# A two-layer hybrid encoder on one core: TensorE's instructions in the order they are emitted, mixer steps spaced by due times, a third PSUM bank for the dense products

## The chip, the cores and the metric

The kernel runs on one core of one Trainium2 chip. The metric is the device time of one execution in microseconds (us); lower is better. Before the change, three runs gave 3186.03, 3193.9 and 3196.83 us, median 3193.9 us. The engines are named as the profile names them: PE is TensorE's matmul, PEld its weight load, DVE VectorE, ACT ScalarE, POOL GpSimd, SP SyncE, which issues the DMAs.

## The reference

Two sequences (called b = 0 and 1 here) of 512 tokens with 1024 features go through two layers (l = 0 and 1) with shared weights. Cut to what matters:

```python
h = rms_norm(x, ln1_g[l])
z = h @ w_in[l]                                  # 1024 -> 2816, in four parts
y = s5(z_s5), hyena(z_hy), rwkv7(z_rw), na(z_na) # four mixers, 256 features each
x = x + concat(rms_norm(y_i, grp_g[l, i])) @ w_out[l]
h = rms_norm(x, ln2_g[l])
x = x + square(relu(h @ w_mlp1[l])) @ w_mlp2[l]  # 1024 -> 4096 -> 1024
```

S5 is a complex diagonal scan in both directions, Hyena two long convolutions done by DFT products, RWKV-7 a delta-rule scan in both directions, the fourth a softmax attention over a neighbourhood of a 8 x 64 grid. All is f32.

## The kernel before

**Dense products.** Features lie on the 128 partitions, the 512 tokens along the free axis. To keep f32 accuracy at the faster matmul type (fp32r), each operand is split into a rounded half `hi` and a rest `lo`, and each 128x128 weight block takes three matmuls of 512 columns (`mm3`, lines 1433 to 1435: hi times hi, hi times lo, lo times hi). A product of `w_in`, `w_out` or `w_mlp1` is 24 such matmuls into one PSUM tile, one of `w_mlp2` is 12. There are 9024 of them. Weights come in blocks of 256 KB through three `hi` buffers and four others (`load_w`): on the first use of a block (sequence 0) it is loaded, cast to `hi` on ACT (L300), the rest `lo` taken by a subtraction on DVE (L301) and written to DRAM; on the second use (sequence 1) block and rest are both loaded, and only the cast on ACT is left (L1417).

**Mixers.** The four mixers of each layer and sequence are many small f32 matmuls and transpositions on PE with chains of DVE, ACT, POOL and DMA work between them. In RWKV (`rw_step`) the longest such chain lies between the transpositions of line 506 and the 32x32 matmuls of line 564 (the inverse of a triangular matrix, lines 508 to 552, on DVE with DMAs in between); a shorter one between line 413 and the matmuls of line 470; then a loop of four serial steps (lines 636 to 687: pw, pu, pS, py). In Hyena (`hy_mixer`) the chain between the forward DFT (L1227) and the inverse (L1277) is the complex arithmetic of line 1196 on DVE and POOL.

**What sets the order.** The program is written as Python generators: one emits the dense stages in turn (w_in of both sequences, then for each layer and sequence w_out, the MLP, the next layer's w_in), two emit mixers. `together` steps them in turn: two steps of each mixer stream for each dense product. The emission order gives each instruction a priority; dense matmuls get a priority number worse by 2000 (`OFF_P`). A list scheduler, which has its own estimate of every instruction's duration, then fixes the order on each engine: it issues whatever it takes to be ready, best priority first. On the chip each engine runs its list strictly in that order.

**Dependences between stages.** w_out of (l, b) needs all four mixers of (l, b), normalised (`group_norm`), split into hi and lo (`take`). Mixers of (l, b) start when the RWKV part of its w_in is done; Hyena and the attention of (0,1), (1,0) and (1,1) start after RWKV and S5 of the same (l, b). After the last w_out only the MLP of (1,1) is left.

**PSUM.** Eight banks: two for dense products (`pd`), three for RWKV, later Hyena (`ra`), two for S5, attention and others (`ma`), one for the norms (`nm`).

## Time and profile before

| | |
|---|---|
| median of three runs | 3193.9 us (3186.03 to 3196.83) |
| profiled execution, its own time | 3182.62 us |
| its span, first to last instruction | 3180.8 us |
| PE busy | 2964.7 us, 93% |
| DVE, ACT, POOL busy | 1935.5, 1128.3, 453.6 us |
| mean granted clock of TensorE | 0.949 |

PE's busy time is the union of matmuls whose ends are modelled and overlap, so it is not PE at its peak. [...] The stages, by the first and last matmul of each: w_in of (0,0) and (0,1) to 469 us; no dense matmul from there to 550; w_out and MLP of (0,0) to 1166; w_in of (1,0) to 1334; w_out and MLP of (0,1), 1340 to 1949; w_in of (1,1) to 2118; w_out and MLP of (1,0), 2145 to 2749; w_out and MLP of (1,1), 2778 to 3176.

### The profile page before, as it was taken

The page shows a single profiled execution, that of the slowest core. Times are in us where ns is not written, and L with a number is a line of the kernel's source. Part 1 is how long each engine was busy: PE and PEld are TensorE (multiplying, and loading weights), DVE is VectorE, ACT ScalarE, POOL GpSimd, SP SyncE. Part 2 cuts the span into 40 slices and gives each one's busy share as a digit, 9 for nine tenths or more (in the row PEclk, how much of TensorE's full clock was granted, in tenths as well). Part 3 has the DMA queues.
Part 4 walks back from the last instruction along what each step waited for, and adds up shares of the span by engine and source line. Part 5 has one row for each costly group of instructions (what it writes and reads, how often), then busy time and mean ns, then how long its engine had stood idle before and what let it go on. Part 6 is the DMA issues. An engine that isn't in the chain of part 4 may idle for free. (4 is left out here: it accounts for less than half of the span.)

```text
span 3180.8 us, 48627 instructions
## 1 busy us (share of the span) xinstructions
PE 2964.7 (93%) x17328; PEld 2317.7 (73%) x17328; DVE 1935.5 (61%) x3909; ACT 1128.3 (35%) x2080; POOL 453.6 (14%) x411
## 2 busy tenths in 40 slices
PE   7978999899999999999999899988999999799999
PEld 5666776677777867777777677866777777588887
DVE  7987783874874697653844527668547467731223
ACT  4333233443332343244332324333433333343332
POOL 3422210200100022211101002213000001100000
PEclk9988997899999999999999999989999999899999
DMA  7577564464565566774764655666646555466666
GB/s 220 184 228 189 172 188 142 139 169 158 163 194 168 188 204 202 240 236 155 207 174 145 182 169 196 218 200 187 177 139 169 174 178 185 155 215 194 194 192 215
DMA packets 491801, 588.70 MB, mean 185 GB/s; under 512 B 188678, under 2 KB 239494, under 8 KB 490536
## 3 DMA queue, kind: packets, MB, share of 16 engines
q1 hardware_dynamic: 491560, 585.59, 60.1%
q8 instruction: 139, 2.28, 0.3%
q14 instruction: 102, 0.84, 0.1%
HBM read 418.34 MB, written 164.22 MB: 183 GB/s over the span
## 5 line engine op out<-in xcount | busy, mean ns | idle before, releaser
L1433 PE MATMUL pd<-m,m 128*128 128x512 f32 x2984 | 1222.0, 410 | 63.8 <-ACT m L300 23.4
L1435 PE MATMUL pd<-m,m 128*128 128x512 f32 x2984 | 1205.7, 405 | 22.5 <-DMA m<-lo 15.7
L1434 PE MATMUL pd<-m,m 128*128 128x512 f32 x2984 | 1205.8, 404 | 1.6 <-DVE m L301 1.4
L1433 PEld LDWEIGHTS pd<-m,m 128*128 128x128 f32 x2984 | 578.3, 194 | 214.2 <-ACT m L300 27.8
L1435 PEld LDWEIGHTS pd<-m,m 128*128 128x128 f32 x2984 | 577.9, 194 | 166.3 <-DMA m<-lo 19.5
L1434 PEld LDWEIGHTS pd<-m,m 128*128 128x128 f32 x2984 | 579.1, 194 | 131.2 <-issue 8.4
L300 ACT CAST m<-m 128x512 fp32r<-128x512 f32 (+1 forms) x400 | 256.4, 644 | 619.9 <-PE pd L1434 220.6
L1417 ACT CAST m<-m 128x512 fp32r<-128x512 f32 x376 | 232.2, 619 | 612.9 <-DMA m<-in_w_mlp 362.4
L301 DVE TENSOR_TENSOR m<-m,m 128x512 fp32r<-128x512 f32 (+1 forms) x400 | 303.1, 761 | 203.4 <-ACT m L300 198.1
L1596 DVE TENSOR_TENSOR m<-pd,m 128x512 f32<-128x512 f32 x224 | 153.9, 688 | 205.4 <-PE pd L1435 204.5
L1578 DVE SCALAR_TENSOR_TENSOR do<-pd,do 128x512 f32<-128x512 f32 x128 | 88.0, 687 | 202.4 <-ACT do L1577 201.9
L1196 DVE TENSOR_TENSOR m<-m,m 128x512 f32<-128x512 f32 (+1 forms) x224 | 125.6, 601 | 6.5 <-PE ma L1375 4.8
L301 DVE TENSOR_TENSOR m<-do,m 128x512 fp32r<-128x512 f32 x128 | 88.2, 689 | 50.0 <-ACT m L300 49.2
L300 ACT CAST m<-do 128x512 fp32r<-128x512 f32 x128 | 79.4, 621 | 98.7 <-DVE do L1578 98.5
L1577 ACT ACTIVATE do<-pd 128x512 f32<-128x512 f32 x128 | 75.9, 593 | 37.6 <-PE pd L1435 37.3
L668 POOL TENSOR_TENSOR rw_se<-rw_st,rw_ec 128x256 f32<-128x256 f32 x24 | 15.8, 659 | 484.1 <-DVE rw_st L669 361.9
L470 PE MATMUL ra<-m,m 64*128 64x128 f32 x512 | 63.1, 308 | 21.8 <-DVE m L454 10.3
L1196 POOL TENSOR_TENSOR m<-m,m 128x512 f32<-128x512 f32 x32 | 49.0, 1534 | 234.7 <-DVE m L1196 77.7
L1457 POOL TENSOR_TENSOR m<-m 128x512 f32<-128x512 f32 x40 | 59.8, 1494 | 152.9 <-ACT m L1456 150.9
L863 POOL TENSOR_TENSOR m<-m,s5p_i 128x256 f32<-128x256 f32 x64 | 61.7, 963 | 135.7 <-DVE m L865 71.4
L678 PE MATMUL ra<-m,m 128*64 128x64 f32 x512 | 78.8, 248 | 1.3 <-DVE m L653 0.9
L470 PEld LDWEIGHTS ra<-m,m 64*128 64x128 f32 x512 | 54.3, 206 | 34.9 <-issue 24.3
(363 smaller groups left out, 3505.6 us busy)
## 6 DMA issues: line engine op xcount, KB each, us to landing
m<-in_w_mlp SPq DMA_DIRECT2D x512, 256.0 KB, 2.9
lo<-m SPq DMA_DIRECT2D x376, 256.0 KB, 2.6
m<-lo SPq DMA_DIRECT2D x376, 256.0 KB, 2.7
m<-in_w_in SPq DMA_DIRECT2D x176, 256.0 KB, 3.2
m<-zr SPq DMA_DIRECT2D x36, 512.0 KB, 4.8
m<-in_w_out SPq DMA_DIRECT2D x64, 256.0 KB, 3.5
m<-in_xT SPq DMA_DIRECT2D x32, 256.0 KB, 4.3
zr<-do SPq DMA_DIRECT2D x32, 256.0 KB, 2.4
```

The costliest lines, as they stand in the source:

```text
L300: self.nc.scalar.copy(out=hi, in_=x)
L301: eng.tensor_tensor(out=lo, in0=x, in1=hi.bitcast(F32), op=SUB)
L470: nc.tensor.matmul(out=pm[q][:, ch - c2, c], lhsT=bk[c][h, ch].rearrange("p a b -> p (a b)"), rhs=ar[c][h, ch].rearrange("p a b -> p (a b) ...
L678: nc.tensor.matmul(out=py[b0:b0 + 64, d, c], lhsT=uv[:, ch, c, q], rhs=sr[:, ch, 2 * c + q], start=st is None, stop=True)
L1196: eng.tensor_tensor(out=o, in0=a, in1=b, op=op)
L1417: nc.scalar.copy(out=hi, in_=raw)
L1433: K.nc.tensor.matmul(out=ps, lhsT=wh, rhs=hh, start=(i == 0), stop=False)
L1434: K.nc.tensor.matmul(out=ps, lhsT=wh, rhs=hl, start=False, stop=False)
L1435: K.nc.tensor.matmul(out=ps, lhsT=wl, rhs=hh, start=False, stop=(i == n - 1))
L1577: nc.scalar.activation(out=r, in_=ps, func=AF.Relu)
L1578: nc.vector.scalar_tensor_tensor(out=r, in0=ps, scalar=0.0, in1=r, op0=MAX, op1=MUL)
L1596: nc.vector.tensor_tensor(out=a, in0=ps, in1=a, op=ADD)
```

## The change

From the first w_out on, the whole PE list is in the order in which the program emits it (`manual_schedule` for PE alone); the other engines are still ordered by the scheduler. What is emitted when is set by `pace`: a clock `K.pe.clock` adds 0.00044 us per column for a dense matmul, 0.00168 us per column for an f32 one and 0.11 us for a transposition. A mixer's `yield 6` now means that its next step is emitted no sooner than 6 us later on that clock. Between steps of mixers, one half of a dense product (12 matmuls, or a whole one of `w_mlp2`) is emitted. The numbers are written at every yield of the mixers, for instance 2 and 11 behind the two halves of RWKV's preparation, 6, 6, 6, 8, 8 and 14 in the long chain, 2, 2 and 2.5 in the serial loop, 6, 5, 5 and 9 in Hyena's arithmetic.

With that, S5, RWKV, Hyena and attention of one (l, b) are started as separate streams (attention after the last part of RWKV has begun, Hyena after RWKV), and steps are cut where one matmul group waits for another engine. Three of four weight subtractions go to POOL instead of DVE. PSUM: `pd` has three banks, `nm` is gone, and the norms of x use `pd`; they are now computed beside the first products of the stage that needs them, which wait for the scale.

```diff
+class PE:
+    def matmul(self, out, lhsT, rhs, **kw):
+        n = int(np.prod(rhs.shape[1:]))
+        self.clock += n * (0.00044 if rhs.dtype == F32R else 0.00168)
+        self.nc.tensor.matmul(out=out, lhsT=lhsT, rhs=rhs, **kw)
...
 def rw_step(K, l, par, g, zr, prep, y, st, M, beside):
...
-        yield
+        yield (2, 11)[c]
...
 def load_w(K, key):
...
-        K.split(hi, lo, raw, nc.vector)
+        K.split(hi, lo, raw, nc.vector if K.nw % LO_V == 0 else nc.gpsimd)
...
 def dense(K, key, h, tag="pd"):
-    w = [load_w(K, key + (kh,)) for kh in range(2)]
     ps = K.p([P, S], tag)
-    mm3(K, ps, [(w[k // 4][0][:, k % 4], w[k // 4][1][:, k % 4], h[k][0], h[k][1]) for k in range(8)])
+    for kh in range(2):
+        wh, wl = load_w(K, key + (kh,))
+        mm3(K, ps, [(wh[:, j], wl[:, j]) + h[4 * kh + j] for j in range(4)], kh == 0, kh == 1)
+        if kh == 0:
+            yield
     return ps
...
 class Stream:
     def step(self, K):
-        for _ in range(self.n):
-            if self.live:
-                K.tc.cur_priority += self.off
-                try:
-                    next(self.gen)
...
+        try:
+            self.ready = K.pe.clock + (next(self.gen) or 0.0)
+        except StopIteration:
+            self.live = False
...
+def pace(K, dense, ordered, *mixers):
+    region = None
+    while dense.live or any(s.live for s in mixers):
+        now = K.pe.clock
+        n = 0
+        for s in mixers:
+            if s.live and s.ready <= now:
+                s.step(K)
+                n += 1
+        if dense.live:
+            dense.step(K)
+        if K.pe.clock == now:
+            K.pe.clock += 0.5
+        if region is None and ordered():
+            region = K.tc.manual_schedule(engines={mybir.EngineType.PE})
+            region.__enter__()
...
-        together(K, Stream(first_stream(), FN, OFF_M), Stream(rwkv_stream(), MIX), Stream(ds, 1, OFF_D))
+        pace(K, Stream(ds), lambda: (0, 0, "out") in done, Stream(first_stream()), Stream(rwkv_stream()))
...
-TB = "nm"
+TB = "pd"
...
-BANKS = {"pd": 2, "ra": 3, "ma": 2, "nm": 1}
+BANKS = {"pd": 3, "ra": 3, "ma": 2}
```

Three places in the lists of the engines. In the changed kernel every matmul is issued from line 203 and every transposition from line 207; a row with 128x512 on a tile `pd` is dense.

**PE, the end of w_in of (1,1), before w_out of (1,0).** Before (the last row is the first matmul of w_out; `ra` with L1277 is Hyena's inverse DFT of (1,0), `ma` with L959 the start of S5 of (1,1)):

```order
L1435 MATMUL pd_20196<-m_18565,m_20191 128x512
L1277 MATMUL ra_16291<-m_15506,m_16238 128x128 x2
...
L296 MATMUL ma_16158<-c_eye_129,rsq_yma_16146 128x128 x4
...
L959 MATMUL ma_20413<-m_20386,m_20409 64x64 x8
L271 MATMUL ra_16361<-c_ones_131,m_16356 128x1 x4
L959 MATMUL ma_20517<-m_20386,m_20513 64x64 x8
L959 MATMUL ma_20634<-m_20386,m_20630 64x64 x8
L296 MATMUL ra_16380<-c_eye_129,rsq_yra_16368 128x128 x4
...
L959 MATMUL ma_20740<-m_20386,m_20736 64x64 x8
L1433 MATMUL pd_20336<-m_18953,m_20320 128x512
```

Now (the fourth row is the first matmul of w_out):

```order
L203 MATMUL pd_19729<-m_18474,m_19759 128x512
L203 MATMUL pd_19779<-m_18188,m_19780 128x512 x2
...
L203 MATMUL pd_19779<-m_18474,m_19799 128x512
L203 MATMUL pd_19832<-m_18995,m_19833 128x512 x2
L203 MATMUL pd_19832<-m_18995,m_19834 128x512
```

The mixer work that stood between the two dense stages has gone to earlier places among the dense matmuls; the stages now follow each other directly.

**PE, the end of the MLP of (1,0), before w_out of (1,1).** Before (L271 and L296 are the norm of a mixer's output):

```order
L1435 MATMUL pd_25333<-m_25136,m_25326 128x512
L271 MATMUL ma_22745<-c_ones_131,m_22740 128x1 x4
L1277 MATMUL ra_22905<-m_22100,m_22848 128x128 x2
...
L296 MATMUL ma_22764<-c_eye_129,rsq_yma_22752 128x128 x4
L271 MATMUL ra_22979<-c_ones_131,m_22974 128x1 x4
L296 MATMUL ra_22998<-c_eye_129,rsq_yra_22986 128x128 x4
L1433 MATMUL pd_25377<-m_25351,m_25365 128x512
```

Now (`ra_25143` and `ra_25181` are Hyena's inverse DFT):

```order
L203 MATMUL pd_25124<-m_25083,m_25117 128x512
L203 MATMUL ra_25143<-m_24008,m_25034 128x128 x2
...
L203 MATMUL pd_25164<-m_24644,m_25156 128x512 x2
...
L203 MATMUL ra_25181<-m_24008,m_25034 128x128 x2
...
L203 MATMUL pd_25309<-m_25083,m_25302 128x512
L203 MATMUL ra_25326<-c_ones_131,m_25244 128x1 x4
L207 MATMUL ra_25346<-c_eye_129,rsq_yra_25333 128x128 x4
L203 MATMUL pd_25367<-m_25353,m_25368 128x512 x2
```

The inverse DFT has moved ahead of five dense products; the two matmul groups of the last norm still stand together, with nothing dense between them or behind them before w_out.

**POOL, the MLP of (0,0), beside the serial loop of RWKV of (0,1).** Before (L668 waits for RWKV's state, L1038 and L1041 are S5's, L1317 the attention's):

```order
L668 TENSOR_TENSOR rw_se_7131<-rw_st_6990,rw_ec_6056 128x256
L668 TENSOR_TENSOR rw_se_7224<-rw_st_7129,rw_ec_6056 128x256
L1038 TENSOR_TENSOR m_7155<-m_7155,m_7154 128x1024
L1041 TENSOR_TENSOR m_7154<-m_7155,m_7154 128x1024
L1317 COPY m_7628<-m_7584 128x256 x4
```

Now (L326 is the subtraction that makes `lo` of a weight block, L699 the line that was L668, L1362 that was L1317):

```order
L326 TENSOR_TENSOR m_9794<-m_9795,m_9793 128x512
L699 TENSOR_TENSOR rw_se_9878<-rw_st_9710,rw_ec_7876 128x256
L326 TENSOR_TENSOR m_9846<-m_9847,m_9845 128x512
L326 TENSOR_TENSOR m_9908<-m_9909,m_9907 128x512
L1362 COPY m_9899<-m_9640 128x256 x4
L326 TENSOR_TENSOR m_9999<-m_10000,m_9998 128x512
L699 TENSOR_TENSOR rw_se_10029<-rw_st_9876,rw_ec_7876 128x256
```

282 of the 376 weight subtractions now stand in POOL's list, between instructions of the mixers.

## Rows read from the trace of the kernel before

**Rows 1.** Page, busy time of each engine.

```profile
PE 2964.7 (93%) x17328; PEld 2317.7 (73%) x17328; DVE 1935.5 (61%) x3909; ACT 1128.3 (35%) x2080; POOL 453.6 (14%) x411
```

**Rows 2.** Windows, two stretches: window, length, busy by engine, PEclk, DMA.

```profile
0.00:550.00 550.00, 486.14 (x3131) 367.14 (x3132) 416.02 (x938) 200.13 (x377) 143.49 (x139) 0.89 0.65 190
550.00:3181.00 2631.00, 2478.59 (x14198) 1950.56 (x14198) 1519.45 (x2971) 928.12 (x1703) 310.10 (x272) 0.96 0.60 184
```

**Rows 3.** Windows by stage, columns PE, PEld, DVE, ACT, POOL, PEclk, DMA, GB/s.

```profile
469.00:550.00 81.00, 72.35 (x715) 52.77 (x716) 34.54 (x87) 27.46 (x71) 4.65 (x7) 0.73 0.54 147
...
642.00:1166.00 524.00, 500.15 (x3215) 391.58 (x3214) 342.98 (x686) 182.95 (x346) 48.21 (x42) 0.98 0.59 177
1166.00:1340.00 174.00, 158.49 (x834) 125.57 (x832) 134.64 (x271) 64.00 (x118) 42.86 (x38) 0.99 0.67 214
...
2118.00:2145.00 27.00, 15.43 (x131) 14.20 (x129) 22.24 (x58) 6.71 (x9) 3.63 (x3) 0.67 0.58 180
...
2749.00:2778.00 29.00, 10.04 (x58) 9.26 (x56) 21.69 (x50) 5.53 (x7) 3.83 (x4) 0.67 0.33 115
...
2824.00:3181.00 357.00, 350.69 (x1549) 289.14 (x1547) 95.50 (x141) 119.12 (x201) 0.00 (x0) 1.00 0.62 198
```

**Rows 4.** Waits of PE from 550 to 3181: total us, times, longest.

```profile
PE ra L564 <- DVE m L551: 18.1, 6, 4.4
PE pd L1433 <- DVE do L1578: 14.3, 9, 2.8
...
PE ra L1277 <- DVE m L1196: 10.5, 3, 8.3
PE ra L470 <- DVE m L454: 10.3, 5, 6.3
...
PE ra L470 <- DVE m L453: 5.8, 3, 4.0
...
PE pd L1433 <- DVE m L1596: 4.8, 4, 3.0
PE pd L1435 <- DVE m L301: 3.0, 3, 1.2
...
PE ra L678 <- DVE m L653: 0.9, 1, 0.9
```

**Rows 5.** Windows, instructions on tiles pd alone: PE, PEld, DVE, ACT, PEclk.

```profile
550.00:3181.00 2631.00, 1971.38 (x7968) 1508.46 (x7968) 300.91 (x436) 94.50 (x160) 0.96 0.60 184
2824.00:3181.00 357.00, 349.85 (x1537) 287.72 (x1535) 61.42 (x89) 23.57 (x40) 1.00 0.62 198
```

**Rows 6.** Timeline before w_out of (1,1).

```profile
2770.18 1.86 PE L271 MATMUL ra<-c_ones,m 128*128 128x1 f32 x8 [5.86 <-DVE m L1534]
...
2777.92 1.22 PE L1433 MATMUL pd<-m,m 128*128 128x512 f32 x2 [2.65 <-ACT m L300]
```

**Rows 7.** Timeline, RWKV's long chain of (1,1), from L506 to L564.

```profile
2418.79 0.90 PE L506 MATMUL ra<-c_eye,m 64*128 64x64 f32 x15
2473.11 1.11 PE L564 MATMUL ra<-m,m 32*32 32x32 f32 x64 [2.14 <-DVE m L551]
```

**Rows 8.** Timeline, Hyena's arithmetic, from L1227 to L1277, twice.

```profile
1991.77 1.02 PE L1227 MATMUL ra<-m,m 128*128 128x256 f32 x4
2022.85 1.39 PE L1277 MATMUL ra<-m,m 128*128 128x128 f32 x11
2716.07 1.13 PE L1227 MATMUL ra<-m,m 128*128 128x256 f32 x4
2758.25 5.63 PE L1277 MATMUL ra<-m,m 128*128 128x128 f32 x32 [8.31 <-DVE m L1196]
```

**Rows 9.** Lines, weight subtraction on DVE; subtractions and sums of that size on POOL.

```profile
L301 DVE TENSOR_TENSOR m<-m,m 128x512 fp32r<-128x512 f32 (+1 forms) x400 | 303.1, 761 | 203.4 <-ACT m L300 198.1 <-DMA zn<-do 2.1 <-DMA lo<-m 1.7
L1457 POOL TENSOR_TENSOR m<-m 128x512 f32<-128x512 f32 x40 | 59.8, 1494 | 152.9 <-ACT m L1456 150.9 <-issue 2.0
L447 POOL TENSOR_TENSOR m<-m,m 128x512 f32<-128x512 f32 x16 | 29.9, 1871 | 14.4 <-DVE m L445 11.5 <-ACT m L431 2.9
```

More of the change, by code (lines that the diff above doesn't have):

```diff
@@ L708, in rw_bonus @@
     yield
+    for c in range(2):
+        p2 = K.p([P, S], "ra")
+        K.pe.matmul(out=p2, lhsT=K.bd, rhs=r[:, c], start=True, stop=True)
+        nc.vector.tensor_tensor(out=r[:, c], in0=p2, in1=v[:, c], op=MUL)
+    M.free(v)
+    yield
     gate = M([P, 2, S])
@@ L740, in rw_out @@
         nc.vector.tensor_tensor(out=y[:, c], in0=gate[:, c], in1=y[:, c], op=MUL)
-        yield
+    rv = rn.rearrange("p (a b c) -> p a b c", a=4, b=2)
+    yield from K.head_bcast([rv[:, :, c] for c in range(2)], M, "ra", finish)
     M.free(bonus, gate)
+    yield 4
 def s5_ops(K, l, M, tag):
@@ L979, in s5_front @@
         M.free(tb, *t)
-        for _ in range(2):
-            yield
+        yield 4
     t = M([P, 8, 128])
@@ L1122, in hy_spectra @@
             M.free(dec)
-        yield
+        yield 4
     M.free(h, lr, w3, ws)
+    yield 2
     pn = K.p([P, S], tag)
     for hf in range(2):
-        nc.tensor.matmul(out=pn, lhsT=K.ones, rhs=tot[:, hf * S:hf * S + S], start=hf == 0, stop=hf == 1)
+        K.pe.matmul(out=pn, lhsT=K.ones, rhs=tot[:, hf * S:hf * S + S], start=hf == 0, stop=hf == 1)
     M.free(tot)
@@ L1344, in weights @@
                 hs = slice(64 * h, 64 * h + 64)
-                nc.tensor.matmul(out=ps[h][:, i], lhsT=q[hs, n * P:n * P + P], rhs=k3[hs, :, span[n]:span[n] + 32],
+                K.pe.matmul(out=ps[h][:, i], lhsT=q[hs, n * P:n * P + P], rhs=k3[hs, :, span[n]:span[n] + 32],
                                  start=True, stop=True)
@@ L1476, in norm_rstd, with w_in @@
     K.nc.scalar.copy(out=r, in_=pb)
-    K.tc.cur_priority += OFF_R
-    return r
-def w_in(K, l, par, h, R, dst, tags):
+    out.append(r)
+def w_in(K, l, par, h, st, M, dst, tags):
     nc = K.nc
     zr, zd, zh, zn = dst
+    Rs = []
+    rs = norm_rstd(K, st, M, Rs)
+    next(rs)
     hp = [(t[:, 0], t[:, 1]) for t in h]
@@ L1519, in s5 @@
         nc.sync.dma_start(out=zd.rearrange("g c t n -> (g c) t n")[i * P:i * P + P], in_=o)
+    R, early = None, []
     for off, n, fn in ((8, 8, rw), (0, 2, s5), (2, 6, hy), (16, 6, na)):
         for i in range(n):
-            fn(i, dense(K, ('w_in', l, off + i), hp, tags.pop() if tags else "pd"))
+            ps = yield from dense(K, ('w_in', l, off + i), hp, tags.pop() if tags else "pd")
+            if R is None:
+                next(rs, None)
+                early.append((fn, i, ps))
+                if Rs:
+                    R = Rs[0]
+                    for f, j, p in early:
+                        f(j, p)
+            else:
+                fn(i, ps)
             yield
@@ L1534, in group_norm @@
     nc.vector.tensor_tensor(out=sq[0], in0=sq[0], in1=sq[1], op=ADD)
-    rn = K.token_rstd(sq[:1], S, K.ones[:, 0:1], 1e-6, tag, sc=1.0 / 256)
+    yield 6
+    rn = yield from K.token_rstd(sq[:1], S, K.ones[:, 0:1], 1e-6, tag, tag, sc=1.0 / 256)
     M.free(*sq)
@@ L1563, in w_out, with mlp @@
     M.free(*(ys.pop(g) for kh in khs for g in HALVES[kh]))
-def mlp(K, l, h, R2, xd, done, M):
+def mlp(K, l, h, st, xd, done, M):
     nc = K.nc
     hp = [(t[:, 0], t[:, 1]) for t in h]
-    hid, acc, xp = {}, [], []
+    hid, acc, xp, R2 = {}, [], [], []
+    rs = norm_rstd(K, st, M, R2, True)
+    next(rs)
     def first(f):
-        ps = dense(K, ('w_mlp1', l, f), hp)
+        ps = yield from dense(K, ('w_mlp1', l, f), hp)
         t = M([P, 2, S], F32R)
@@ L1607, in mlp @@
     for f in range(32):
-        first(f)
+        yield from first(f)
+        next(rs, None)
         yield
@@ L1643, in both @@
         for s in streams:
-            s.step(K)
-        yield
+            if s.live and s.ready <= K.pe.clock:
+                s.step(K)
+        yield max(0.0, min([s.ready for s in streams if s.live], default=0.0) - K.pe.clock)
+def pace(K, dense, ordered, *mixers):
[5 more added lines that the diff above has]
+            if s.live and s.ready <= now:
+                s.step(K)
+                n += 1
[6 more added lines that the diff above has]
+            region.__enter__()
+    if region is not None:
+        region.__exit__(None, None, None)
 def chain(*gens):
@@ L1695, in into @@
             ys[l, b] = {}
-            for i, _ in enumerate(w_in(K, l, pars[l], h, R, zs[l, b], FIRST[:] if l + b == 0 else None)):
-                if i == 7:
+            for i, _ in enumerate(w_in(K, l, pars[l], h, st, DM, zs[l, b], FIRST[:] if l + b == 0 else None)):
+                if i >= 15:
                     done.add(("zr", l, b))
-                    if b == 0 and l and len(ys[l - 1, 1]) == 4:
-                        take(l - 1, 1)
-                    if b == 1 and l and len(ys[l, 0]) == 4:
-                        take(l, 0)
+                    other = (l, 0) if b else (l - 1, 1)
+                    if l and len(ys[other]) == 4 and other not in taken:
+                        take(*other)
                 yield
@@ L1760, in na @@
             yield from na_mixer(K, l, pars[l], zs[l, b][3], y, M, tag)
[L1761 removed]
+            yield from group_norm(K, pars[l], 3, y, tag, M)
             ys[l, b][3] = y, M
```

318 lines of the change are left out of this document (170 added, 148 removed).

## The prediction

> **What bounds the kernel now.** I read the page's busy times first [rows 1]: PE is busy in 93% of the span, every other engine in 61% or less, so the order on PE decides. Then the windows. The change orders PE by hand only from the first w_out on, at 550 us, so I split the span there [rows 2]. Behind 550 lie 2631 us with PE busy for 2478.6: 152 us idle, and a granted clock of 0.96, which is 0.04 x 2631 = 105 us of clock withheld. These 257 us are what a better order can win; before 550 the scheduler still orders PE. The windows by stage show where it lies [rows 3]: the last stage, dense work alone, has no idle time beyond its tail and a clock of 1.00, the long MLP stages with mixers have 0.98, and two short stretches in front of a w_out have 0.67 with PE busy 15.4 of 27 and 10.0 of 29 us. The waits of PE name what ends the idle time [rows 4]: chains of DVE work inside the mixers (L564, L470, L1277) and dense matmuls that wait for a PSUM bank to be read (L1578, L1596).
>
> How long a dense matmul needs: 1537 in 349.85 us, 0.228 us each [rows 5]. All 7968 behind 550 would need 1814 us; they were busy for 1971 [rows 5]. The 157 us between are clock, changes between mixer and dense work, and waits too short to show as idle.
>
> **The change part by part.** The number of matmuls is the same in both lists, so only idle time, clock and placement count. Each term is for the time behind 550.
>
> *Stage ends, -29.* Before w_out of (1,0) mixers are left over; now nothing stands there. The stretch is 27 us, its PE work at full clock is 15.4 x 0.67 = 10 us and is paid elsewhere: -17. Before w_out of (1,1) the inverse DFT moves ahead of five dense products, but the last norm still stands alone: from its first matmul to w_out it took 7.7 us [rows 6], and I keep 10 of the 29; with 10.0 x 0.67 = 7 us of PE work that is -12. Bounds: -39 (nothing is left) and 0 (other work is late there).
>
> *Third bank, -16.* The dense matmuls waited 14.3 us for L1578 and 4.8 for L1596 [rows 4], 19 in all; a third tile hides them. The norms now take banks of this tag too, so I leave 3. Bounds -19 and +10.
>
> *RWKV's long chain, -18.* From the last transposition (about 2419.7) to the first L564 the chip needed 53.4 us, 2.1 of them idle [rows 7]. Between the two, PE's list held 188, 223, 174, 164, 200 and 192 dense matmuls in the six instances, 37 to 51 us at 0.228: too few, hence 18.1 us of waits in all six [rows 4]. Now it holds 216, 252, 228, 264, 240 and 264, 49 to 60 us, and up to 14 us of mixer matmuls besides. What is late next is the chain's own end, which has room. Bounds -18 and +20 (if the chain lasts 57 us).
>
> *RWKV's preparation, -12.* L470 waited 10.3 and 5.8 us [rows 4], 2 us each time. The PE work in front of it was 5 to 10 us and is now 10 to 13. Bounds -16 and 0.
>
> *Hyena's arithmetic, +10.* Two instances took 30 and 41 us from L1227 to L1277, the second with an 8.3 us wait [rows 8]; now the list holds 33 to 34 us of PE work there, six times. I take two instances late by 5. Bounds 0 and 6 x 7 = +42.
>
> *Serial loop, +8.* Between its steps stood 21 dense matmuls on average and now mostly 12, 2.7 us. The trace shows 0.9 us of wait behind L653 with the longer distance [rows 4]. With some 60 steps, and the row's 0.9 for one in seven, +8; bounds 0 and 60 x 0.9 = +54.
>
> *Subtractions on POOL, +10.* 282 move. One takes 0.761 us on DVE and would take about 1.494 as the POOL group of that shape does [rows 9], 0.73 more. That is hidden where the rest is ready in time: of all these, PE waited only 3.0 us for L301 in three places [rows 4]. I charge 0.73 us to fourteen of them; if that cover were gone it would be 282 x 0.73 = +206. In exchange DVE sheds 282 x 0.761 = 215 of its 1935 us, so the other bound is -20.
>
> [...]
>
> *Short waits and mixing, -25.* Before, a mixer's matmul could break into a product after any dense matmul; now only between halves. Of the 157 us above, about 80 are clock (0.04 x 1971). I take a third of the other 77. Bounds -60 and 0.
>
> *Clock, -45.* The two short stretches account for 0.33 x 56 = 18 of the 105 us; 87 are left. The stages in which PE waits little run at 0.98 and 0.99, the last at 1.00 [rows 3]. If all mixer stages, some 2230 us, came to 0.985, 33 of the 87 would stay: -54; new waits take 9 back. Bounds -87 and 0.
>
> *Before 550, 0 +- 20.* The emission differs, the scheduler still orders. 33 of the 44 subtractions of the first w_in leave a busy DVE, 416 of 550 us [rows 2], but S5's preparation now shares the dense banks.
>
> Sum: -29 - 16 - 18 - 12 + 10 + 8 + 10 - 25 - 45 = -117 us. Against the profiled execution's 3182.6 that is 3066; it ran 11 us faster than the median of the runs, 3193.9, from which the forecast is 3077.
>
> **The rivals.** *All waits gone.* Every chain has room and the clock follows: 142 of the 152 us, the 87 of clock and 10 of mixing go: 3193.9 - 239 = 2955. For it: six of six L564 waits are covered. Against: Hyena's 33 us stands against 41 measured, and the stretch from 469 to 550 has PE busy 72 of 81 us at a clock of only 0.73 [rows 3], so mixers alone keep it low. [...]
>
> *Late rests from POOL (slower).* POOL runs its list in order, and the subtractions now stand behind instructions that wait for RWKV's state. If the rest of a block comes late by 0.73 us each time, the dense work of sequence 0 pays: 206 in place of 10, which is 3077 + 196 = 3273. It decides from 117 / 282 = 0.4 us a block. Against: one block feeds 12 matmuls, 2.7 us, and four buffers give three of these as slack; POOL is busy in 14% of the span [rows 1].
>
> *Chains longer than their due times (slower).* Hyena late by 7 us six times and the loop by 0.9 in every step, +96 in place of 18, and the clock stays at 0.96 since PE waits as often: 3077 + 78 + 45 = 3200.
>
> *Gain eaten up.* Half of that: the old waits go, new ones of the same size come with the shorter distances in the loop, and the clock stays: about 3165.
>
> **How the numbers follow.** The forecast's case, 3020 to 3140: 0.5. All or most waits gone, below 3020: 0.2. Gain eaten up, 3140 to 3184: 0.1; to within 0.3% of 3193.9, which is about what a measurement of this kernel can tell from no change, 0.06. Slower 0.14: POOL 0.05, chains 0.09. Faster is 0.5 + 0.2 + 0.1 = 0.8. The range 2955 to 3195 leaves out little below and the slower cases above; the likeliest case alone has 3020 to 3140.
>
> **What would show it.** Right: no stretch without dense matmuls before w_out of (1,0), a short one before w_out of (1,1); L564 and L470 out of the list of waits; no dense matmul waiting for L1578's successor; PEclk behind the first w_out near 0.98; DVE busy some 200 us less, POOL some 420 more. Wrong: L1277's successor with waits of several us in most instances; dense matmuls of sequence 0 waiting for POOL; idle time behind the first w_out above 100 us; or a first w_out much later or earlier than 550.

## The result, and the profile after

The changed kernel takes 3324.6 us (median of four runs) against 3190.0 us for the kernel before beside it: a ratio of 1.042, 95% interval 1.0387 to 1.0453. It is 135 us slower, where the prediction had 117 us faster. The profiled execution has a span of 3323.3 us.

The page's busy times of the changed kernel, as in [rows 1]:

```profile
PE 2993.9 (90%) x17328; PEld 2327.0 (70%) x17328; DVE 1878.6 (57%) x3627; ACT 1138.8 (34%) x2084; POOL 820.6 (25%) x693
```

The number of matmuls is the same and PE is busy only 29 us longer; 113 of the 142 us between the spans are idle time. POOL has 367 us more. By the prediction DVE sheds 215 us with the moved subtractions; it shed 57, since its other work became slower.

The windows of the changed kernel, cut at its first w_out, which now starts at 606 us; they answer to [rows 2], with the same columns:

```profile
0.00:606.00 606.00, 512.55 (x3253) 381.88 (x3253) 428.44 (x938) 209.33 (x388) 200.99 (x179) 0.86 0.60 175
606.00:3323.00 2717.00, 2481.34 (x14076) 1945.14 (x14076) 1450.16 (x2690) 929.44 (x1697) 619.62 (x514) 0.93 0.58 178
```

The first w_out is 56 us later. Behind it PE is busy as long as before, but idle for 236 us instead of 152, and the granted clock is 0.93 instead of 0.96. The stages, as in [rows 3] (from the end of w_in of sequence 1 to the first w_out; the first MLP; the next w_in; the stretches without dense matmuls before w_out of (1,0) and of (1,1); the last stage):

```profile
512.00:606.00 94.00, 82.41 (x746) 58.57 (x745) 49.47 (x137) 34.06 (x88) 7.50 (x11) 0.72 0.39 104
731.00:1317.00 586.00, 534.48 (x3324) 413.98 (x3323) 353.95 (x642) 199.51 (x394) 205.65 (x180) 0.93 0.55 166
1317.00:1508.00 191.00, 165.87 (x656) 122.66 (x654) 112.96 (x160) 68.31 (x96) 81.23 (x63) 0.90 0.60 195
2299.00:2306.00 7.00, 0.69 (x4) 0.23 (x2) 6.93 (x5) 0.62 (x2) 2.10 (x2) 0.88 0.90 213
2909.00:2920.00 11.00, 2.75 (x16) 2.14 (x15) 7.84 (x19) 4.46 (x6) 0.00 (x0) 0.63 0.64 215
2971.00:3323.00 352.00, 346.13 (x1531) 285.83 (x1529) 93.81 (x138) 117.08 (x198) 0.00 (x0) 1.00 0.62 199
```

The first MLP and the w_in behind it went from 0.98 and 0.99 to 0.93 and 0.90. The stretches before w_out of (1,0) and (1,1), 27 and 29 us before the change, are 7 and 11 us. The last stage, dense work alone, is what it was. What PE waits for behind the first w_out, as in [rows 4] (all matmuls now have line L203, all transpositions L207):

```profile
PE ma L203 <- DMA m<-s_sB: 37.4, 12, 13.1
PE ra L203 <- DVE m L482: 24.0, 4, 7.5
PE pd L203 <- ACT m L325: 23.5, 12, 6.5
PE pd L203 <- DVE m L1515: 18.2, 7, 6.3
PE pd L203 <- DVE m L1666: 11.8, 4, 6.4
PE ma L203 <- DVE m L1397: 11.4, 3, 5.8
PE ma L203 <- POOL m L1079: 8.4, 3, 5.1
...
PE pd L203 <- POOL m L326: 6.1, 8, 1.5
```

The old waits are nearly gone, as forecast: no line names the last step of RWKV's long chain or Hyena's arithmetic, and the MLP's squaring (L1648) has one wait of 0.9 us. Others have grown or are new: S5's operator blocks from DRAM (s_sB), RWKV's preparation (L482), weights and x on their way to the dense products (L325, L1515), the attention's scores (L1397), the last step of S5's activation function on POOL (L1079). The first of them stood in the list of the kernel before too, as its third longest line, which [rows 4] leaves out:

```profile
PE ma L959 <- DMA m<-s_sB: 11.7, 5, 4.9
```

A simple measure serves for what follows: the time at which the n-th dense product starts (us from the span's start; one product here is one 128x512 matmul on a tile `pd` or `ra`: the 9024 dense ones, 16 of RWKV's and, where the third bank is shared, 8 of S5's). I counted it in the traces of the runs told below. Number 1152 lies in the first w_out, 3456 in w_out of sequence 1, layer 0.

```
product   before  changed  a_dve  a_dve_noorder  spacing_only  unspaced0_hyena  best_with_order
  768       357     349     353       355            350            350             355
 1152       594     695     688       665            646            615             658
 3456      1378    1574    1555      1502           1507           1455            1485
 7680      2865    3006    2974      2863           2878           2835            2973
 span      3181    3323    3291      3180           3194           3152            3290
```

By product 3456 the changed kernel is 196 us late, at the end 142: the loss falls into the first half, and the second half is 54 us faster than before.

### The profile page after: what moved, and what is told of

Its sections match the earlier page's. It is cut to its first block, busy times and chain, and to the rows that moved or that the text cites. A ratio compares the mean times of both kernels' runs of the same rounds, so it can differ in the third digit from the quotient of the medians.

```text
span 3323.3 us, 48638 instructions
## 1 busy us (share of the span) xinstructions
PE 2993.9 (90%) x17328; PEld 2327.0 (70%) x17328; DVE 1878.6 (57%) x3627; ACT 1138.8 (34%) x2084; POOL 820.6 (25%) x693
## 5 line engine op out<-in xcount | busy, mean ns | idle before, releaser
L203 PE MATMUL pd<-m,m 128*128 128x512 f32 (+2 forms) x9248 | 2309.4, 407 | 136.1 <-ACT m L325 38.0
L203 PEld LDWEIGHTS pd<-m,m 128*128 128x128 f32 (+2 forms) x9248 | 1745.1, 194 | 580.8 <-issue 51.4
L326 POOL TENSOR_TENSOR m<-m,m 128x512 fp32r<-128x512 f32 x282 | 390.4, 1385 | 800.0 <-ACT m L325 768.9
L325 ACT CAST m<-m 128x512 fp32r<-128x512 f32 (+1 forms) x400 | 257.6, 645 | 728.5 <-PE pd L203 332.3
L203 PE MATMUL ra<-m,m 32*32 32x32 f32 (+5 forms) x3448 | 267.6, 251 | 42.8 <-DVE m L482 24.0
L1666 DVE TENSOR_TENSOR m<-pd,m 128x512 f32<-128x512 f32 x224 | 153.8, 688 | 248.1 <-PE pd L203 247.7
L203 PE MATMUL ma<-m,m 128*64 128x128 f32 (+10 forms) x1584 | 196.5, 322 | 94.0 <-DMA m<-s_sB 37.4
L1648 DVE SCALAR_TENSOR_TENSOR do<-pd,do 128x512 f32<-128x512 f32 x128 | 88.2, 689 | 338.7 <-ACT do L1647 338.4
L203 PEld LDWEIGHTS ra<-m,m 32*32 32x32 f32 (+4 forms) x3448 | 201.6, 151 | 106.7 <-issue 47.2
L203 PEld LDWEIGHTS ma<-m,m 128*64 128x64 f32 (+4 forms) x1584 | 117.8, 159 | 149.2 <-issue 55.7
L326 DVE TENSOR_TENSOR m<-m,m 128x512 fp32r<-128x512 f32 (+1 forms) x118 | 100.0, 848 | 117.0 <-ACT m L325 112.1
L1236 DVE TENSOR_TENSOR m<-m,m 128x512 f32<-128x512 f32 (+1 forms) x224 | 147.2, 707 | 0.0
L326 DVE TENSOR_TENSOR m<-do,m 128x512 fp32r<-128x512 f32 x128 | 92.4, 722 | 64.2 <-ACT m L325 63.0
L325 ACT CAST m<-do 128x512 fp32r<-128x512 f32 x128 | 79.6, 622 | 105.6 <-DVE do L1648 105.3
L1515 DVE SCALAR_TENSOR_TENSOR m<-m,par,m 128x512 fp32r<-128x512 f32 x64 | 64.3, 1014 | 31.3 <-ACT m L1514 31.2
L1236 POOL TENSOR_TENSOR m<-m,m 128x512 f32<-128x512 f32 x32 | 48.9, 1529 | 110.0 <-DVE m L1236 68.1
L203 PE MATMUL ra<-m,rw_st 64*64 64x64 f32 x448 | 75.7, 251 | 0.0
L560 DVE TENSOR_TENSOR m<-m 128x1024 f32<-128x1024 f32 x32 | 66.0, 2063 | 11.2 <-DMA m<-m 5.3
```

The costliest lines, as they stand in the source:

```text
L203: self.nc.tensor.matmul(out=out, lhsT=lhsT, rhs=rhs, **kw)
L325: self.nc.scalar.copy(out=hi, in_=x)
L326: eng.tensor_tensor(out=lo, in0=x, in1=hi.bitcast(F32), op=SUB)
L560: nc.vector.tensor_tensor(out=tm, in0=x[:, i:i + 4].unsqueeze(2).to_broadcast([P, 4, 16, 16]), in1=z.rearrange("p j k -> p k j").unsqueeze ...
L1236: eng.tensor_tensor(out=o, in0=a, in1=b, op=op)
L1515: nc.vector.scalar_tensor_tensor(out=h[:, 1], in0=x, scalar=g, in1=h[:, 0].bitcast(F32), op0=MUL, op1=SUB)
```

## Experiments

Ratios are to the kernel before on the same chip, with 95% intervals; "changed" is the changed kernel. Times in us are medians. The kernel before took 3183 to 3196 us on the chips used, so a difference between runs on two chips can be some us off; where that matters it is taken from the ratios.

### The parts, undone one by one

**a_dve**: the subtractions of the weights back on VectorE.

```
-LO_V, OFF_W, OFF_P = 4, 0, 2000
+LO_V, OFF_W, OFF_P = 1, 0, 2000
```

> The changed kernel with all 400 weight subtractions back on VectorE; order of TensorE, spacing and banks stay. Theory P (POOL): the 282 subtractions that went to GpSimd cost the loss, because they run beside VectorE's operations on SBUF and slow them (the 128x512 sums of the Hyena mixer 601 to 707 ns, the 128x128 ones of S5 323 to 483 ns, the small RWKV ones 301 to 379 ns), so that the mixers' steps come late where TensorE now waits for them in a fixed order: 3190 to 3230 us. Theory O (order): TensorE held in the order of emission waits wherever a mixer is later than the estimate that spaced it, whoever does the subtractions: 3290 to 3340 us. Theory S (spacing): the steps are spaced so that mixer work of the first two stages falls late, with or without the fixed order: 3290 to 3340 us too.

3291.5 us, 1.0313 (1.0284 to 1.0343): 33 us of the loss are theirs, the larger part is not.

**b_pool**: the kernel before, with that part alone.

```
-        K.split(hi, lo, raw, nc.vector)
+        K.split(hi, lo, raw, nc.vector if K.nw % LO_V == 0 else nc.gpsimd)
```

> The kernel before with one thing of the change alone: three of four subtractions of the weights on GpSimd. Theory P: VectorE's operations on SBUF slow beside them here too, and RWKV's and S5's chains with them: 3230 to 3320 us. Theories O and S: 3170 to 3200 us, as before, since TensorE is not bound to an order by hand and fills a late step with dense products.

3208.8 us, 1.0059 (1.0037 to 1.0081): a loss of 19 us (by the ratio) in the kernel before as well, between the two expectations. Why it costs is in the lines of VectorE. In the changed kernel (its POOL line first):

```profile
L326 POOL TENSOR_TENSOR m<-m,m 128x512 fp32r<-128x512 f32 x282 | 390.4, 1385 | 800.0 <-ACT m L325 768.9 <-DMA m<-in_w_mlp 19.3 <-DMA lo<-m 7.0
L1666 DVE TENSOR_TENSOR m<-pd,m 128x512 f32<-128x512 f32 x224 | 153.8, 688 | 248.1 <-PE pd L203 247.7
L901 DVE TENSOR_TENSOR m<-m,m 128x128 f32<-128x128 f32 x128 | 57.3, 483 | 6.2 <-POOL m L899 5.2
L1236 DVE TENSOR_TENSOR m<-m,m 128x256 f32<-128x256 f32 x128 | 71.5, 599 | 0.0
```

and in a_dve, which differs in the subtractions' engine alone:

```profile
L1666 DVE TENSOR_TENSOR m<-pd,m 128x512 f32<-128x512 f32 x224 | 154.0, 687 | 229.6 <-PE pd L203 229.2
L901 DVE TENSOR_TENSOR m<-m,m 128x128 f32<-128x128 f32 x128 | 36.8, 322 | 5.1 <-POOL m L899 4.1
L1236 DVE TENSOR_TENSOR m<-m,m 128x256 f32<-128x256 f32 x128 | 61.2, 513 | 0.0
```

The sum that takes one operand from PSUM lasts 688 and 687 ns. Those with both operands in SBUF go from 322 to 483 ns and from 513 to 599. S5's sums of 128x128 show it in b_pool as well: 323 ns before, 431 there. The subtraction itself took 1385 ns, near the 1494 assumed. PE waited for it 6.1 us behind the first w_out. The cost is on the mixers' chains: from a_dve to the changed kernel PE's waits on the mixers' tiles (ra, ma) rise from 150 to 180 us, while those on tiles pd fall from 155 to 142.

**a_noorder**: no order by hand anywhere, the scheduler orders TensorE. **a_late**: the order by hand only from w_out of sequence 1 on.

```
-        pace(K, Stream(ds), lambda: (0, 0, "out") in done, Stream(first_stream()), Stream(rwkv_stream()))
+        pace(K, Stream(ds), lambda: False, Stream(first_stream()), Stream(rwkv_stream()))                  (a_noorder)
+        pace(K, Stream(ds), lambda: (0, 1, "out") in done, Stream(first_stream()), Stream(rwkv_stream()))  (a_late)
```

> The changed kernel without TensorE's order by hand at any place: the scheduler sets it, as in the kernel before; subtractions, spacing and banks stay. Theory O: the waits for mixers on TensorE between 606 and 1592 us (some 130 us, against 58 in the kernel before) fall back: 3190 to 3240 us. Theory P: the mixers are still late: 3280 to 3340 us. Theory S: 3300 to 3400 us, since the emission is what puts the mixers' steps where they are.

> The changed kernel with the order by hand from w_out of sequence 1 of layer 0 on, and not from the first w_out. From there on the changed kernel was 33 us faster than before (1731 against 1764 us to the end), and 175 us later at that place. Theory O: the 85 to 120 us lost between the first w_out and there shrink to 0 to 40: 3210 to 3250 us. Theories P and S: they stay, 3290 to 3340 us.

a_noorder 3237.8 us, 1.0152 (1.0116 to 1.0187): the order by hand costs 87 us, the largest part. a_late 3284.4 us, 1.0303 (1.0269 to 1.0337): neither range, and 47 us above a_noorder. The order costs in the later stages too, where I had taken the changed kernel to be winning.

**a_dve_noorder**: both undone.

> The changed kernel with all subtractions on VectorE and without the order by hand; spacing, merged streams and banks stay. Undone alone, the subtractions gave back 33 us and the order 87. If the two act apart: 3195 to 3215 us, and spacing with banks then costs some 10 to 20 us by itself. If the order is what makes late mixers cost (theory O with P as its feeder), the subtractions are worth little without it: 3225 to 3245 us. If spacing with banks is the gain of the sum on record: 3130 to 3170 us.

3190.5 us, 0.9986 (0.9971 to 1.0001): as before the change, and just under the first range. So with subtractions on VectorE the order costs 101 us (3291.5 to 3190.5). Undone one at a time the two parts give back 33 and 87 us, together 134: they act nearly apart.

**a_banks_back**: the changed kernel with two banks for the dense products and one for the norms and S5's first work. **spacing_only**: the same banks in a_dve_noorder, so that only the spacing, the merged streams and the finer steps remain. **b_banks**: the kernel before with the shared banks alone.

```
-TB = "pd"
-BANKS = {"pd": 3, "ra": 3, "ma": 2}
+TB = "nm"
+BANKS = {"pd": 2, "ra": 3, "ma": 2, "nm": 1}
...
-            yield from both(K, Stream(s5_ops(K, 0, MS, "pd")), Stream(hy_spectra(K, 0, MW, "ma")))
+            yield from both(K, Stream(s5_ops(K, 0, MS, "nm")), Stream(hy_spectra(K, 0, MW, "ma")))
```

> The changed kernel with the PSUM banks of before (two for the dense products, one for the norms, S5's operators of layer 0 and S5's product of the first sequence); order by hand, spacing, subtractions stay. Theory B (sharing a bank couples the dense products to S5's chain and to the norms, because banks are handed round in the order of emission): alone in the kernel before the shared banks cost 91 us; where the mixers are spaced the products stand further ahead, so half of that: 3260 to 3290 us. If the third bank is a gain, as the prediction has it: 3330 to 3350 us. If spacing already takes the coupling away: 3315 to 3330 us.

> Of the change only the spacing by estimates with the streams merged and the finer steps: subtractions on VectorE, TensorE's order from the scheduler, PSUM banks of before. With shared banks this is 3190.5 us. Theory B: 3130 to 3170 us. If sharing does no harm once the mixers are spaced: 3185 to 3210 us.

> The kernel before with one thing of the change alone: the norms' PSUM bank goes to the dense products, which then share three banks with the norms and S5's operators. By the prediction on record the third bank is worth 16 us: 3170 to 3182 us. If the dense products never wait for a bank that matters, or the norms now hold one up: 3185 to 3205 us.

a_banks_back 3330.1 us, 1.0438 (1.041 to 1.0465): not distinguishable from the changed kernel. spacing_only 3198.3 us, 1.0018 (0.9994 to 1.0042): some 8 us behind shared banks, intervals overlapping. In these two kernels the third bank is worth little. But b_banks takes 3286.3 us, 1.0295 (1.027 to 1.032): 91 us slower, which no theory of mine had. What PE waits for in it from 20 to 590 us:

```profile
PE pd L271 <- DVE s5p_sm L759: 25.3, 1, 25.3
PE ra L470 <- DVE m L453: 24.0, 4, 14.2
PE pd L922 <- DVE m L865: 16.7, 1, 16.7
```

Two matmuls on tiles of the dense products' tag, one of a norm (L271) and one of S5's operators (L922), wait 25.3 and 16.7 us for VectorE's work on S5's operators. The windows of the dense tiles show the effect from 221 to 469 and to 589 us (in the kernel before, then in b_banks):

```profile
221.00:469.00 248.00, 145.92 (x530) 105.09 (x528) 15.79 (x22) 0.00 (x0) 0.89 0.65 185
469.00:589.00 120.00, 20.54 (x76) 15.14 (x77) 4.66 (x7) 0.00 (x0) 0.77 0.49 135
```

```profile
221.00:469.00 248.00, 61.36 (x286) 46.90 (x280) 6.29 (x10) 3.39 (x9) 0.68 0.46 125
469.00:589.00 120.00, 58.72 (x284) 42.19 (x285) 8.18 (x12) 2.54 (x4) 0.89 0.49 150
```

With the banks shared, product 768, in the w_in of sequence 1, started at 589 us instead of 357. My reading is that it stood behind S5's tiles in the rotation of the banks. In the changed kernel, where the mixers are emitted later against the products, product 768 started at 349.

### Why the order by hand costs 100 us

a_dve and a_dve_noorder are emitted alike and differ in the order by hand alone. Summed over the lists of waits, PE's waits for dense products (tiles pd, which hold norms and S5's first work as well) are 155 and 164 us, those on the mixers' tiles (ra, ma) 150 and 55. Longest lines of the mixers' tiles in a_dve:

```profile
PE ma L203 <- DMA m<-s_sB: 23.1, 9, 6.9
PE ra L203 <- DVE m L482: 21.0, 4, 7.4
...
PE ma L203 <- DMA m<-s_sC: 14.7, 8, 5.3
...
PE ma L203 <- DVE m L1397: 9.9, 4, 4.9
```

and of a_dve_noorder the two that are left at the head:

```profile
PE ma L203 <- DMA m<-s_sB: 6.9, 9, 1.4
...
PE ra L203 <- DVE m L578: 5.3, 3, 3.2
```

The windows from product 1152 to 7680, a_dve:

```profile
688.00:2974.00 2286.00, 2111.26 (x12385) 1642.67 (x12386) 1361.61 (x2623) 808.45 (x1494) 277.41 (x257) 0.94 0.59 180
```

and a_dve_noorder:

```profile
665.00:2863.00 2198.00, 2088.91 (x12474) 1632.22 (x12473) 1367.67 (x2673) 805.73 (x1495) 300.90 (x260) 0.97 0.62 188
```

Between them lie 88 us: 66 of idle time (175 against 109) and 22 of busy time at the lower clock. With PE's list fixed the scheduler orders the other engines differently too (by line and tile, 1415 of VectorE's 3909 instructions have the same place in both kernels), so these us belong to the edit as a whole. What happens at one such place shows in the timeline of the changed kernel, rows of PE, VectorE and the DMA queue of SP, beside the first w_out:

```profile
643.57 0.69 PE L203 MATMUL ma<-m,m 128*64 128x64 f32 x16
...
647.13 0.98 PE L203 MATMUL ra<-m 64*128 64x256 f32 x12
...
657.01 0.68 DVE L482 TENSOR_TENSOR m<-m,m 64x512 f32<-64x512 f32 x1
657.61 0.62 DVE L1015 TENSOR_TENSOR m<-m,m 128x64 f32<-128x64 f32 x4
657.76 0.32 SPq L989 DMA_DIRECT2D m<-s_tb  x1
658.26 0.32 SPq L987 DMA_DIRECT2D m<-s_sB  x1
661.19 1.12 PE L203 MATMUL ma<-m,m 128*64 128x64 f32 x16 [13.08 <-DMA m<-s_sB]
662.24 1.22 PE L203 MATMUL pd<-m,m 128*128 128x512 f32 x2
```

S5's step loads its block (L987) and multiplies with it in the same step, without an estimate between; the load stood in SP's queue until 658.26. The transfer is the smaller part, 2.9 us from there to the product: the semaphore that released the load is that of L1015, the last VectorE instruction of S5's step before, after which its memory is given back (`M.free`), and the load ahead of it (L989) waited for VectorE's L482, in RWKV's preparation. The estimate behind a step of S5 is 4 us (`yield 4`); from one product of S5 to the next it took 17.6. PE idled 13.08 us in front of the second, with dense products right behind it in its list. In a_dve_noorder the same chain is no shorter, 19.9 us from product to product, and its load waits for L1015 too, but PE has dense products in between and S5's product waits for nothing:

```profile
649.51 0.69 PE L203 MATMUL ma<-m,m 128*64 128x64 f32 x16
...
659.43 9.59 PE L203 MATMUL pd<-m,m 128*128 128x512 f32 x41 [0.86 <-DVE m L326]
664.01 0.62 DVE L1015 TENSOR_TENSOR m<-m,m 128x64 f32<-128x64 f32 x4
...
664.66 0.32 SPq L987 DMA_DIRECT2D m<-s_sB  x1
...
669.37 0.69 PE L203 MATMUL ma<-m,m 128*64 128x64 f32 x16
```

**a_estimates16, a_estimates06**: all estimates times 1.6 or 0.6 from the first emitted w_out on (the second run has 0.6 in the same place).

```
-            self.ready = K.pe.clock + (next(self.gen) or 0.0)
+            gap = next(self.gen) or 0.0
+            self.ready = K.pe.clock + gap * (1.6 if (0, 0, "out") in K.done else 1.0)
```

> The changed kernel with every estimate of the spacing times 1.6 from the first emitted w_out on; order by hand, subtractions, banks stay. With the order by hand the mixers' products wait 150 us for operands (subtractions on VectorE), without it 55, the dense products 155 and 164. Theory E (the estimates are shorter than what the chains take, so a fixed order puts a product where its operand is not ready): mixers' waits fall from 180 to under 110 us and the time to 3230 to 3280 us. Rival R (the chains then end later than the dense products that need them, and the waits move to the first products of w_out): 3310 to 3380 us. Rival F (a fixed order waits for whichever engine queue happens to be late, at any spacing): 3290 to 3330 us.

> The changed kernel with every estimate times 0.6 from the first emitted w_out on. Times 1.6 gave 3435 us, with the waits where the mixers ran past the dense products, and no fewer waits beside them. Theory F: the estimates set where the waits are, not whether; mixers' waits of 160 to 260 us and 3300 to 3400 us. Theory E: with shorter estimates more products stand before their operands: over 3380 us. If the chains as emitted were too long at 1.0 already (rival R): 3250 to 3300 us.

3435.2 us, 1.0778 (1.0739 to 1.0818), above every range, and 3387.0 us, 1.0607 (1.0587 to 1.0627), which theories F and E both allow. The mixers' waits are 287 us and 258, against 180 at 1.0. With 1.6, as I read it, the mixers run past the products that could hide them. Two late stretches by its windows, with 115 and 82 us idle (the longest line of waits in them is that of a mixer's last norm, 37.6 us in two waits):

```profile
1964.00:2513.00 549.00, 434.46 (x2567) 340.35 (x2566) 326.50 (x645) 172.34 (x324) 121.84 (x104) 0.86 0.53 160
2513.00:3121.00 608.00, 526.32 (x3078) 412.86 (x3077) 291.36 (x529) 187.75 (x358) 145.93 (x119) 0.88 0.47 148
```

So neither of these two scales lets the fixed order pass. That single estimates, set from measured chains, would, was not tried. The clock on which the estimates run is off as well: it charges an f32 matmul 0.00168 us per column, 1.72 us for four of 256 columns, and four such took 1.02 us [rows 8]. No run tells what that costs.

### The first stretch, and a faster kernel

**a_hyena**: Hyena of the first sequence is emitted behind its own spectra, not also behind S5's operators. **spacing_hyena**: the same edit in spacing_only. **a_unspaced0** (on a_noorder), **unspaced0_banks_back**, **unspaced1_banks_back** (both on spacing_only): spacing out of force until the first w_out, or until that of sequence 1. **unspaced0_hyena**: unspaced0_banks_back with the edit of a_hyena.

```
-            yield from both(K, Stream(s5_ops(K, 0, MS, "pd")), Stream(hy_spectra(K, 0, MW, "ma")))
-            yield from until(("z", 0, 0))
-            yield from chain(hyena(0, 0, MW, "ma"), na(0, 0, MW, "ma"))
+            yield from both(K, Stream(s5_ops(K, 0, MS, "pd")), Stream(chain(
+                hy_spectra(K, 0, MW, "ma"), until(("z", 0, 0)), hyena(0, 0, MW, "ma"), na(0, 0, MW, "ma"))))
...
-            self.ready = K.pe.clock + (next(self.gen) or 0.0)
+            gap = next(self.gen) or 0.0
+            self.ready = K.pe.clock + gap if SPACED in K.done else 0.0
```

> The changed kernel with one edge taken out of the emission: the Hyena mixer of sequence 0, layer 0 is emitted behind its own spectra and no longer also behind S5's operators, which end at 273 us in the kernel before and at 319 in the changed one. Order by hand, spacing, subtractions, banks stay. If that edge is what makes the first w_out late (Hyena's arithmetic starts at 376 us against 289): first w_out at 545 to 575 us and 3265 to 3295 us in all. If the first w_out waits for the attention mixer or the VectorE queue as a whole: 3310 to 3335 us.

> The changed kernel without the order by hand, and with the spacing out of force until the first w_out is emitted (every mixer is stepped at each step of the dense stream until then; afterwards the estimates hold). Theory S: the 80 us that the kernel without order is behind the kernel before at dense product 1152 come from the spacing of the first stretch: 3160 to 3200 us, first w_out near 550 instead of 606 us. Against it (the merged streams, the subtractions or the banks delay the first w_out): 3225 to 3250 us.

> As spacing_only, with Hyena of the first sequence emitted behind its own spectra and not also behind S5's operators. In the changed kernel this edge brought product 1152 50 us forward (640 against 695 us), of which 6 us were left at the end. If they were lost to the order by hand: 40 to 50 us under spacing_only, 3090 to 3120 us where that is 3150. If later stages are bound by something else (the mixers' own queue on VectorE): within 15 us of spacing_only.

> As spacing_only, with the spacing out of force until the first w_out is emitted. With shared banks the unspaced first stretch had the dense product 768 at 480 us against 351, so it was coupled to S5's tiles, and no gain could show. Theory S with B: the first stretch is then that of the kernel before (product 1152 near 594 us and not 665), the rest that of spacing (1680 us from product 3456 to the end against 1803): 3090 to 3130 us. If the first stretch is late by the merged streams or finer steps: 3140 to 3190 us.

> As unspaced0_banks_back (3166 us), but the spacing out of force until the w_out of sequence 1, layer 0 is emitted. From product 1152 to 3456 the kernel before takes 784 us and all kernels with spacing 848 to 881; from 3456 on it takes 1803 and they 1680 to 1691 without order by hand. Theory S (early mixers' work pulled forward by the spacing, and worth its gain only later): 3456 products done by 1390 to 1420 us, 3090 to 3120 us in all. Theory D (what is gained later is the mixers' work that was done earlier, a debt and not a gain): 3150 to 3190 us, with the stretch after 3456 back at 1750 to 1800 us.

> As unspaced0_banks_back, with Hyena of the first sequence also emitted without waiting for S5's operators. The edge was worth 14 us where the first stretch is spaced (3198 to 3184). If the two add: 3145 to 3158 us. If both cure the same delay: 3160 to 3172 us.

- a_hyena: 3318.7 us, 1.0394 (1.0372 to 1.0415). Product 1152 came 55 us sooner (640 against 695), and only some 6 us were left at the end. The time lies in the second range, but not for its reason, since the first w_out did come sooner.
- a_unspaced0: 3253.1 us, 1.0176 (1.0152 to 1.02). Product 768 started at 480 us, as late as in b_banks or nearly; with the banks of before (and the subtractions on VectorE) it is 359, in unspaced0_banks_back. That the shared banks hold the products up where mixers are stepped ahead fits both.
- spacing_hyena: 3183.8 us, 0.9972 (0.9953 to 0.9992), 14 us under spacing_only.
- unspaced0_banks_back: 3166.3 us, 0.9928 (0.9903 to 0.9954), 32 us under spacing_only; product 1152 at 624 us, not at 594.
- unspaced1_banks_back: 3164.2 us, 0.993 (0.9909 to 0.9952). Product 3456 only at 1489 us, so keeping the spacing off does not bring the early pace of the kernel before back; the time is theory D's, the late stretch (to product 7680 in 1355 us against 1487 before) is not.
- unspaced0_hyena: 3157.4 us, 0.9912 (0.9878 to 0.9946). It beats the kernel before by 0.9% and the changed one by 5%; that a_hyena's edit adds to unspaced0_banks_back (0.9928) is not shown.

In all kernels with the new emission, product 3456 is 77 us late or more, and the stretch from there to product 7680 83 us or more faster unless the order is by hand (1404 us in a_unspaced0, 1487 before). The late gain is in part mixers' work that was done early: between the products 3456 and 7680 PE ran 8242 matmuls in the kernel before, 7564 in unspaced1_banks_back. How much of the late gain is more than that is open.

**best_with_order**: unspaced0_hyena with the order by hand from the first w_out on (the line of a_noorder put back). **best_three_banks**: unspaced0_hyena with three banks shared by products and norms, S5's first work on the mixers' tag "ma".

> unspaced0_hyena (3157 us; subtractions on VectorE, banks of before, first stretch unspaced) with TensorE's order by hand from the first w_out on. Theory F (a fixed order costs by itself, whatever stands around it, because no dense product can be put before a mixer's product whose operand is late): +80 to +110 us, 3235 to 3270, with 80 to 100 us more of mixers' waits. Against it (the order cost so much only beside the late first stretch, the shared banks or the subtractions on GpSimd): 3150 to 3190 us.

> unspaced0_hyena with three banks for the dense products and the norms, but S5's operators and product of the first sequence in the mixers' banks, so that no chain of a mixer stands in the dense products' rotation. If the third bank is worth what shared banks gave beside the spacing (8 us): 3143 to 3153 us. If S5 in the mixers' two banks holds up Hyena's spectra: 3160 to 3190 us.

best_with_order: 3293.2 us, 1.0303 (1.0267 to 1.0339): some 125 us by the ratios for the order alone, more than theory F had. Its waits on the mixers' tiles and the norms' (ra, ma, nm) sum to 215 us against 93, its dense waits are 109 against 107. best_three_banks: 3186.8 us, 0.9974 (0.996 to 0.9987), some 20 us behind unspaced0_hyena by the ratios. A third bank bought by putting S5 elsewhere does not pay either; whether b_banks lost its 91 us to S5's tiles or to the norms stays open.

## Why the prediction was wrong

The loss adds up along a path of single steps: spacing and merged streams +6 (spacing_only), shared banks -8, order by hand +101, subtractions +33: 132 of 135 us.

- **The step that failed first: "These 257 us are what a better order can win".** The sum took PE's waits of the old order one by one and asked whether the new order covers each. For the waits that it named this went mostly as forecast: RWKV's long chain had 18.1 us in six waits [rows 4] and has no line now (its next link, L600 and L602, has 4.7), Hyena's arithmetic none (forecast +10), the serial loop one wait of 5.0 us (L672, forecast +8). For waits that a fixed order opens or lengthens elsewhere it had no term beyond these and 9 us of clock, and gave no reason. S5's blocks waited 11.7 us before, 8.6 of them in the stretch before w_out of (1,0), which the term for the stage ends counts, and wait 37.4 now; the attention's scores and S5's activation, 11.4 and 8.4 now, had no line in that list. In all the order by hand costs 101 us, with 150 us of mixers' waits instead of 55. That this is the order and not the mixers' place is shown by a_dve and a_dve_noorder, and again by unspaced0_hyena and best_with_order.
- **RWKV's preparation, -12.** 16.1 us of waits before [rows 4]; L482 and L481 now have 24.0 and 5.0. Its distance of "10 to 13" us in the list was not enough.
- **Clock, -45, and short waits and mixing, -25.** The clock term rested on waits going away. The clock went from 0.96 to 0.93 behind the first w_out: by these rounded rows 0.07 x 2717 = 190 us are withheld instead of 105. The dense tiles, 0.247 us a matmul before [rows 5], now need 0.251, from this row of the changed kernel:

```profile
606.00:3323.00 2717.00, 2019.00 (x8040) 1540.22 (x8040) 302.00 (x442) 97.54 (x166) 0.93 0.58 178
```

Whether the mixing term came true below that clock is open: 0.247 x 0.96 is 0.237 and 0.251 x 0.93 is 0.233, but the second row holds small matmuls of the norms too.

- **Subtractions, +10.** Measured +33 with the order by hand, +47 without, +19 in the kernel before. The term priced a late operand on PE, and that part was right: 6.1 us of waits for POOL. (Its 0.761 us on DVE is a mean that takes in 24 wider tiles [rows 9]; the 376 of this shape alone took 0.731.) It left out VectorE's instructions beside POOL's work: from a_dve to the changed kernel S5's sums of two SBUF operands went from 322 to 483 ns (L901), Hyena's from 513 to 599 (L1236, 128x256), while the sum with a PSUM operand was not slowed (L1666, 687 and 688 ns).
- **Before 550, 0 +- 20.** The first w_out is 56 us late. The spacing and the edge to S5's operators are part of the delay: product 1152 is at 646 us with the spacing, at 606 without that edge, at 624 unspaced, at 615 with both, and at 594 before. The fixed order is not in force in these kernels.
- **Third bank, -16.** The mechanism held: behind the first w_out the 14.3 us behind the squaring are 0.9 now, though the 4.8 of L1596 are 11.8 (L1666). From spacing_only to a_dve_noorder, which differ in the banks alone, these two waits fall from 23.7 to 1.3 us over the whole span, and those for x at the start of a stage (L1514, L1515) rise from 8.0 to 18.9. On the whole the bank gave some 8 us, within the noise; the bound of +10 was far too narrow, as b_banks shows with 91 us where mixers are emitted ahead of products.
- **Stage ends, -29.** This term was right in kind. The stretches before w_out of (1,0) and (1,1) went from 27 and 29 us to 7 and 11; with the 10 and 7 us of PE work that the prediction counts as paid elsewhere, that is some 20 us won (27 - 7 - 10 and 29 - 11 - 7). The last norm still stands alone before w_out of (1,1), as it said.

Of its own signs of being wrong two came: 236 us idle behind the first w_out, above the 100, and a first w_out at 606 us instead of 550.

The rival "chains longer than their due times" came nearest in kind, at 3200 us; it counted Hyena and the serial loop, and the chains that came late were S5's (17.6 us against an estimate of 4) and RWKV's preparation. The rival of late rests from POOL did not happen: dense products waited 6.1 us for POOL.

## To carry over

A list of waits shows what the present order failed to hide, not what it hides. Before an order is fixed by hand, ask of every operand what must end before it, since nothing slips in front of a product that stands fixed: PE idled 13.08 us before one of S5's, with dense products right behind it. A wait put down to a DMA can be one for another engine: S5's load was issued only at 658.26 us, when VectorE had released its memory, and the product followed 2.9 us later. Work moved to an idle engine is to be priced with its neighbour's instructions, here 483 ns instead of 322 for S5's sums on VectorE. A bank given to a pool that two streams share cost 91 us in one kernel and nothing that could be measured in another, which emits the two otherwise.

## What the runs showed of the hardware

Two groups of VectorE's sums of two SBUF operands became slower when GpSimd had the subtractions (a_dve against the changed kernel): 322 to 483 ns for the 128x128 sums of S5, 513 to 599 for the 128x256 ones of Hyena's arithmetic. Those of L1666, which read PSUM, took 687 and 688 ns.

The granted clock and PE's idle time in three windows: 0.97 in a_dve_noorder with 109 us of 2198 idle, 0.94 in a_dve with 175 of 2286, 0.86 in a stretch of a_estimates16 with 115 of 549. Idle time is not all of it: w_in of (1,0) in the kernel before had 0.99 with 16 us of 174 idle [rows 3], and from 512 to 606 us in the changed kernel, with small matmuls of mixers and hardly any on tiles pd (3 us), the clock was 0.72 with 12 us of 94 idle. A mean hides short stretches: in the kernel before the clock was 0.50 from 472 to 492 us and 1.00 from 494 to 504.
